# Sixteen gate projections in pairs with seven block products, in a one-core mixer block

## The chip, the cores and the metric

The kernel runs on one core of a Trainium2 chip. The metric is the device time of one execution in microseconds (us). A core has TensorE (PE in the rows; its weight loads are PEld), VectorE (DVE), ScalarE (ACT), GpSimd (POOL) and SyncE (SP), which issues most DMAs. Each engine runs its own instructions in order and waits for others by semaphores.

## The reference, cut to what matters

One transformer block on 512 tokens of width 1024, all in float32: a norm, one wide input projection, four mixers (a gated delta rule, a latent attention, a gated linear attention and an attention with forgetting), then the gates, and an MLP of width 4096. The change is in the gates:

```python
merged = 0
for i in range(4):
    gate = sigmoid(h @ w_gate[i] + b_gate[i])          # h: 512 x 1024, w_gate[i]: 1024 x 1024
    merged = merged + gate * (branches[i] @ w_branch_up[i])
x = x + rms_norm(merged @ w_out, norm_mix_post)
u = relu(rms_norm(x, norm_mlp_pre) @ w_mlp_in)         # 1024 x 4096
x = x + rms_norm((u * u) @ w_mlp_out, norm_mlp_post)
```

## The kernel before

**Numbers in two parts.** Every float32 factor of a projection is split into a high part (rounded, `fp32r`) and a low part (the rest): `split` (L157) has ScalarE cast the high part (L158) and VectorE subtract it from the source (L161). `mm3` (L257) then makes three matmuls: high by high, high by low, low by high. A projection (`proj`) of 128 output rows is 8 blocks of 128 inputs x 3 = 24 matmuls of 512 tokens.

**Tiles and buffers.** `raw_cols` loads 128 columns of a weight as 128 x 1024 (tag `raw`, four buffers); `w_split` splits them into tags `whi` and `wlo`, three buffers each. `h` is kept as `hh` and `hl`, its two parts. PSUM has two banks `acc` and six banks b0 to b5, which `ps_sm` gives out in a ring. `tmp` (L341) has four buffers of 128 x 512.

**Order.** The program is written as one sequence; a scheduler orders each engine's instructions ahead of the run, by readiness and then by place in the sequence (`tc.high_priority()` lifts a few). A tile gets a buffer of its tag when an earlier tile has let go of it.

**The gates.** `gates` (L589) makes 32 gate projections: number n is branch n % 4, rows 128 x (n // 4). The result leaves PSUM as Exp (L595), then Ln and Exp in place (L596, L597): a sigmoid. There are 11 gate buffers, so gates run up to 11 ahead of their use; two are made early, others fill TensorE's gaps in the attention parts. The loop over m = 0 to 7 (L1031) calls `gates(4 * m + 11)`, makes the branch projection of rows m (a `w_split` of `w_branch_up` and 24 matmuls, six for each branch, into four banks), multiplies each by its gate (VectorE, L1042), adds the four products on POOL (L1044, L1046) and splits the sum into `mh` and `ml`. A round from m = 2 to m = 5 is thus four gate projections and one branch projection.

**The MLP's first projection.** From its seventh block on it goes in pairs of 128-row blocks. A pair is a product of a 2 x 2 block matrix of weights (A11, A12, A21, A22, each 128 rows by 512 inputs) with a 2 x 2 block matrix of inputs (B, each 512 inputs by 256 tokens). Instead of eight block products it makes seven, of sums of blocks (Strassen's scheme in Winograd's form). `w_sums` (L1176) splits A11 and A12, then A22 into a tile `yw` of tag `y` (two buffers), then makes the four sums S1 to S4 in place in the raw weights (L1148), and splits these. `part` (L1172) makes one block product of 4 x 3 = 12 matmuls of 256 tokens. The sums T1 to T4 of the input blocks are made once, in place in `h2f`, a float32 copy of the input.

Of the kernel before, what the change touches and what calls it, by code (L numbers as in the profile page):

```python
# [121 lines left out]
def hybrid_mixer_kernel(ctx, tc, I, out):  # L122
# [891 lines left out]

    mpool = ctx.enter_context(tc.tile_pool(name="mpool", bufs=1, side="right"))

    def m_tile(name, dt):
        return mpool.tile([P, KD, S], dt, name=name, tag="mbig", bufs=2)

    mh = m_tile("mh", F32R)  # L1020
    ml = m_tile("ml", F32R)

    br_hl = {}
    for n, (i, p) in enumerate((i, p) for i in (0, 3, 2, 1) for p in range(2)):
# [2 lines left out]
        split(hi, lo, brT[i][p])  # L1027
        br_hl[i, p] = hi, lo

    banks["ring"] = ("b0", "b1", "b2", "b3", "b4", "b5")  # L1030
    for m in range(KD):  # L1031
        gates(4 * m + sum(NGATE))
        rv = raw_tile().rearrange("p (k c) -> p k c", k=KD)
        sp.dma_start(out=rv, in_=I["w_branch_up"][0].rearrange("i (k p) c -> p (i k) c", p=P)[:, :, P * m:P * m + P])
        hi, lo = w_split(rv)
        for i in range(4):
            ps = ps_sm()
            for k in range(2):
# [14 lines left out]
    def big2(name, dt):  # L1053
        return ph2.tile([P, KD, S], dt, name=name, tag="big2", bufs=2)
# [77 lines left out]
        act_sq(first[a][0], a)  # L1132

    KH = KD // 2
    B = [[h2f[:, KH * i:KH * i + KH, 256 * j:256 * j + 256] for j in range(2)] for i in range(2)]

    def rows_split(src, where):  # L1140
        wp, wb, tag = where
        hi = wp.tile([P, 1024], F32R, name="thi", tag=tag + "hi", bufs=wb).rearrange("p (k c) -> p k c", k=KH)
        lo = wp.tile([P, 1024], F32R, name="tlo", tag=tag + "lo", bufs=wb).rearrange("p (k c) -> p k c", k=KH)
        split(hi, lo, src)
        return hi, lo

    def diff(out, a, b, op=ALU.subtract):
        dve.tensor_tensor(out=out, in0=a, in1=b, op=op)  # L1148
# [12 lines left out]
    u2 += [big2("u2", F32)] + [m_tile("u2b", F32) for _ in range(2)]
    block = lambda i, j: tuple(z[:, KH * i:KH * i + KH, 256 * j:256 * j + 256] for z in (h2h, h2l))

    ring8 = [lambda: ps_sm("b0"), lambda: ps_sm("b1"), lambda: ps_sm("b2"), lambda: ps_sm("b3"), lambda: ps_sm("b4"),
             lambda: ps_sm("b5"), ps_acc, ps_acc]
    turn = [0]

    def bank():
        turn[0] += 1
        return ring8[(turn[0] - 1) % 8]()[:, 0:256]  # L1170

    def part(ps, w, t, start=True):  # L1172
        for k in range(KH):
            mm3(ps, w[0][:, k], w[1][:, k], t[0][:, k], t[1][:, k], start and k == 0, k == KH - 1)

    def w_sums(m):  # L1176

        r = [raw_cols(w1, (m + i) * P) for i in range(2)]
        A = [[v[:, KH * i:KH * i + KH] for i in range(2)] for v in r]

        def wt(name):
            return [wpool.tile([P, 1024], F32R, name="w" + z, tag="w" + z, bufs=3).rearrange("p (k c) -> p k c", k=KD)
                    for z in ("hi", "lo")]

        x = wt("x")
        split(x[0], x[1], r[0])
        z_ = ph2.tile([P, D], F32R, name="yw", tag="y", bufs=2).rearrange("p (z k c) -> p z k c", z=2, k=KH)
        z = (z_[:, 0], z_[:, 1])
        split(z[0], z[1], A[1][1])
        diff(A[1][1], A[1][0], A[1][1], ALU.add)  # L1190
        diff(A[1][0], A[0][0], A[1][0])
        diff(A[0][0], A[1][1], A[0][0])
        diff(A[0][1], A[0][1], A[0][0])
        got = []
        for pair in ((A[0][0], A[1][1]), (A[1][0], A[0][1])):
            e = wt("e")
            for i, src in enumerate(pair):
                ks = slice(KH * i, KH * i + KH)
                split(e[0][:, ks], e[1][:, ks], src)
                got.append((e[0][:, ks], e[1][:, ks]))  # L1200
        A11, A12 = [(x[0][:, KH * i:KH * i + KH], x[1][:, KH * i:KH * i + KH]) for i in range(2)]
        S2, S1, S3, S4 = got
        return A11, A12, z, S1, S2, S3, S4

    sz = lambda name: ph2.tile([P, 256], F32, name=name, tag="sz", bufs=4)
    for m in range(NPLAIN, DFF // P, 2):
        A11, A12, A22, S1, S2, S3, S4 = w_sums(m)
        o = [[u2[(m + i) // 8][:, (m + i) % 8, 256 * j:256 * j + 256] for j in range(2)] for i in range(2)]
        p1, p6, p5, p7, p3 = [bank() for _ in range(5)]
        part(p1, A11, block(0, 0))  # L1210
        s1 = sz("s1")
        with tc.high_priority():
            act.copy(out=s1, in_=p1)
        part(p6, S2, T2)
        sa = sz("sa")
        with tc.high_priority():
            diff(sa, p6, s1, ALU.add)
        part(p5, S1, T1)
        sb = sz("sb")
        with tc.high_priority():  # L1220
            diff(sb, p5, sa, ALU.add)
        part(p1, A12, block(1, 0), False)
        act.activation(out=o[0][0], in_=p1, func=AF.Relu)
        part(p7, S3, T3)
        with tc.high_priority():
            diff(o[1][1], p7, sb, ALU.add)
        part(p3, S4, block(1, 1))
        diff(o[0][1], p3, sb, ALU.add)
        part(p7, A22, T4, False)
        diff(o[1][0], p7, sa, ALU.add)  # L1230
        for i, j in ((0, 1), (1, 1), (1, 0)):
            act.activation(out=o[i][j], in_=o[i][j], func=AF.Relu)
# [81 lines left out]
```

## Time and profile before

| | us |
|---|---|
| median of 3 runs | 876.04 (874.59 to 876.36) |
| profiled execution | 875.75 |
| its span | 874.0 |
| TensorE busy in the span | 858.1 |
| VectorE busy | 529.9 |
| ScalarE busy | 441.4 |
| POOL busy | 75.6 |

The span runs from the first instruction to the last; the rest of the profiled execution's time lies around it. A busy share is an average over stages with different limits. A matmul's duration in the trace overlaps that of the next one, so the rate is read from the distance of two starts. In a row, `[x <-Y]` is idle time of that engine before the instruction, and what ended it.

### The profile page before, as it was taken

To read this page: it belongs to the slowest core of one execution; us is meant where nothing else is said; L and a number is where in the kernel's file an instruction comes from. 1 tells how busy PE (TensorE), PEld (TensorE's weight loads), DVE (VectorE), ACT (ScalarE), POOL (GpSimd) and SP (SyncE) were. 2 spreads that over 40 slices of the span, in tenths; PEclk is the share of its full clock that TensorE was granted. 3 is DMA by queue.
4 is the path that set the end of the run, shared out by engine and by line. 5 is a ranking of instruction groups with operands and counts; after the bars stand their busy time and mean duration, and the time that the engine had idled before them with its cause. 6 is when DMAs were issued, how large, how long until landed. Compare 5 with 4: busy or idle time off the path is not lost.

```text
span 874.0 us, 12382 instructions
## 1 busy us (share of the span) xinstructions
PE 858.1 (98%) x4875; PEld 728.8 (83%) x4875; DVE 529.9 (61%) x882; ACT 441.4 (50%) x788; POOL 75.6 (9%) x87
## 2 busy tenths in 40 slices
PE   7999999999999999999999999999999999999996
PEld 6988778897777777888888779999999988888885
DVE  5479698445886684444336469888888633333334
ACT  5444762433995866444453356466666632222222
POOL 3200020110000002222105100300000000000000
PEclk9999999999999999999999999999999999999999
DMA  8334153601212103333333822333344433333202
GB/s 267 86 97 118 51 95 106 145 25 49 61 49 74 48 25 97 96 97 97 97 96 97 258 56 73 87 108 97 97 109 129 148 122 97 96 97 97 73 1 96
DMA packets 123674, 83.33 MB, mean 95 GB/s; under 512 B 19472, under 2 KB 115744, under 8 KB 123616
## 3 DMA queue, kind: packets, MB, share of 16 engines
q1 hardware_dynamic: 117696, 77.03, 30.7%
q10 hardware_dynamic: 5696, 4.73, 1.8%
q8 instruction: 38, 0.62, 0.3%
q0 software_dynamic: 224, 0.79, 0.3%
q14 instruction: 20, 0.16, 0.1%
HBM read 79.63 MB, written 2.88 MB: 94 GB/s over the span
## 4 chain that ended last, share of the span: by engine, by line
PE 86%; DVE 6%; DMA 2%; ACT 2%; POOL 2%; issue 1%; ACTq 0%; SPq 0%; DVEq 0%; POOLq 0%
PE acc L259 41%; PE b L259 34%; PE b L819 2%; DMA raw<-in_w_mlp_in_dram 2%; DVE wlo L161 2%; DVE qkvT L442 1%; PE b L849 1%; PE b L840 1%; PE b L648 1%; ACT whi L158 1%; DMA raw<-in_w_in_dram 1%; POOL gate L1044 1%; POOL wlo L161 1%; PE b L495 1%; PE b L294 1%
## 5 line engine op out<-in xcount | busy, mean ns | idle before, releaser
L161 DVE TENSOR_TENSOR wlo<-raw,whi 128x1024 fp32r<-128x1024 f32 (+1 forms) x173 | 190.2, 1109 | 146.6 <-ACT whi L158 146.3
L158 ACT CAST whi<-raw 128x1024 fp32r<-128x1024 f32 (+1 forms) x175 | 159.7, 921 | 211.7 <-PE acc L259 143.6
L259 PE MATMUL acc<-hh,wlo 128*128 128x512 f32 x368 | 145.9, 396 | 0.8 <-DVE wlo L161 0.8
L259 PE MATMUL acc<-hh,whi 128*128 128x512 f32 x368 | 146.1, 397 | 0.0
L259 PE MATMUL acc<-hl,whi 128*128 128x512 f32 x368 | 145.1, 394 | 0.0
L259 PEld LDWEIGHTS acc<-hh,wlo 128*128 128x128 f32 x368 | 69.2, 188 | 16.6 <-issue 1.6
L259 PEld LDWEIGHTS acc<-hh,whi 128*128 128x128 f32 x368 | 69.2, 188 | 14.9 <-issue 1.6
L259 PEld LDWEIGHTS acc<-hl,whi 128*128 128x128 f32 x368 | 69.2, 188 | 13.7 <-issue 0.4
L259 PE MATMUL b<-whi 128*128 128x512 f32 x192 | 74.7, 389 | 0.0
L259 PE MATMUL b<-wlo,whi 128*128 128x512 f32 x192 | 74.7, 389 | 0.0
L259 PE MATMUL b<-whi,wlo 128*128 128x512 f32 x192 | 74.6, 390 | 0.0
L259 PE MATMUL b<-h2l,whi 128*128 128x256 f32 x168 | 47.7, 284 | 0.0
L259 PE MATMUL b<-h2h,wlo 128*128 128x256 f32 x168 | 47.6, 283 | 0.0
L259 PE MATMUL b<-h2h,whi 128*128 128x256 f32 x168 | 47.5, 283 | 0.0
L259 PEld LDWEIGHTS b<-whi,wlo 128*128 128x128 f32 x192 | 36.0, 188 | 7.8 <-DVE wlo L161 0.3
L259 PEld LDWEIGHTS b<-wlo,whi 128*128 128x128 f32 x192 | 36.1, 188 | 7.5
L259 PEld LDWEIGHTS b<-whi 128*128 128x128 f32 x192 | 36.0, 188 | 7.3
L1044 POOL TENSOR_TENSOR gate<-gate 128x512 f32<-128x512 f32 x16 | 22.6, 1416 | 198.3 <-DVE gate L1042 198.3
L1148 DVE TENSOR_TENSOR raw<-raw 128x512 f32<-128x512 f32 x52 | 37.3, 717 | 0.9
L259 PE MATMUL b<-thi,whi 128*128 128x256 f32 x116 | 32.8, 283 | 0.0
L259 PE MATMUL b<-tlo,whi 128*128 128x256 f32 x116 | 32.8, 283 | 0.0
L259 PE MATMUL b<-thi,wlo 128*128 128x256 f32 x116 | 32.8, 283 | 0.0
(366 smaller groups left out, 1853.0 us busy)
## 6 DMA issues: line engine op xcount, KB each, us to landing
raw<-in_w_gate_dram SPq DMA_DIRECT2D x32, 512.0 KB, 4.1
raw<-in_w_mlp_in_dram SPq DMA_DIRECT2D x32, 512.0 KB, 4.9
raw<-in_w_mlp_out_dram SPq DMA_DIRECT2D x32, 512.0 KB, 3.5
raw<-in_w_in_dram SPq DMA_DIRECT2D x23, 512.0 KB, 3.8
raw<-in_w_branch_up_dram SPq DMA_DIRECT2D x8, 512.0 KB, 4.1
raw<-in_w_out_dram SPq DMA_DIRECT2D x8, 512.0 KB, 3.6
x_t<-in_x_dram SPq DMA_DIRECT2D x4, 512.0 KB, 7.9
x<-in_x_dram ACTq DMA_DIRECT2D x1, 2048.0 KB, 12.0
```

The source lines that it names most:

```text
L158: c = act.copy(out=hi, in_=src)
L161: eng.tensor_tensor(out=lo, in0=src, in1=hi.bitcast(F32), op=ALU.subtract)
L259: pe.matmul(out=ps, lhsT=a, rhs=b, start=first and i == 0, stop=last and i == 2, skip_group_check=True)
L294: pe.transpose(out=ps[:, k * P:(k + 1) * P], in_=(src if late else sq)[:, ks], identity=ident)
L442: dve.scalar_tensor_tensor(out=y[:, sh:], in0=ps[:, 0:S - sh], scalar=vec(V_CONV + 6 * j + m), in1=y[:, sh:], op0=ALU.mult, op1=ALU.add)
L495: made.append(pe.matmul(out=ps2[e][:, js], lhsT=qkvT[2 + p][r, js], rhs=qkvT[rhs_i + p][r, js], start=j == 0, stop=j == NT - 1, skip_group ...
L648: pe.matmul(out=pv[:, j], lhsT=av[h][:, j], rhs=src[:, j], start=j == 0, stop=j == NT - 1, skip_group_check=True)
L819: pe.matmul(out=ps[:, at_[j]:at_[j] + n], lhsT=qT[e][0:rows, j * P:n], rhs=kT[e][0:rows, 0:n], start=j == js[0], stop=j == js[-1], skip_gr ...
L840: pe.transpose(out=pst[:, k * P:(k + 1) * P], in_=pr[:, k * P:(k + 1) * P], identity=ident)
L849: made.append(pe.matmul(out=psb[C * e:C * e + C, i * P:(i + 1) * P], lhsT=vt(k, 2 * p + e), rhs=pts[e][:, at_[j] + k * P:at_[j] + (k + 1) ...
L1044: pool.tensor_tensor(out=g, in0=g, in1=gts[4 * m + i - 1], op=ALU.add)
L1148: dve.tensor_tensor(out=out, in0=a, in1=b, op=op)
```

## The change

Gates 15 to 30 are made in eight pairs, (15, 16), (17, 18) and so on, with the same scheme as the MLP: the two gates' weights are the two rows of blocks, `hh` and `hl` the inputs. Gates 0 to 14 and gate 31 stay as they were. The functions of the scheme are moved ahead of both uses and shared.

- Once, before the loop over m: `hf` = `hh` + `hl` (four additions of 128 x 1024), four sums of its blocks, four splits into eight tiles `gt`. `hf` and, after it, `ml` share the one buffer of tag `mbig1`; `mh` has `mbig0`.
- For a pair: two raw weights; A11 and A12 split together, A22 split into `zg`, four sums in place, S1 to S4 split; seven products. `zg` is one pair of `tmp` tiles for all pairs, as are the intermediate results `s1`, `sa` and `sb`.
- A pair's gates leave as Exp in three pieces, then Ln and Exp as before.
- Branch projections take banks b3 to b5 in a ring; pairs take b0, b1, b2 and the two `acc`. In the MLP the pairs take the same fixed banks, where they went round all eight.
- In the MLP the four sums of input blocks are made before their splits, where they alternated; the last two relus of a pair's second half-result are one.

```diff
+GPLAIN = 15
+    def strassen_sums(f):
+        B = [[f[:, KH * i:KH * i + KH, 256 * j:256 * j + 256] for j in range(2)] for i in range(2)]
+        diff(B[0][0], B[0][1], B[0][0])
+        diff(B[0][1], B[1][1], B[0][1])
+        diff(B[1][1], B[1][1], B[0][0])
+        diff(B[1][0], B[1][0], B[1][1])
+        return B[0][0], B[0][1], B[1][1], B[1][0]
+    def strassen_weights(r, z_tile):
+        A = [[v[:, KH * i:KH * i + KH] for i in range(2)] for v in r]
...
+        x = wt()
+        split(x[0], x[1], r[0])
+        z = z_tile()
+        split(z[0], z[1], A[1][1])
+        diff(A[1][1], A[1][0], A[1][1], ALU.add)
+        diff(A[1][0], A[0][0], A[1][0])
+        diff(A[0][0], A[1][1], A[0][0])
+        diff(A[0][1], A[0][1], A[0][0])
+        for pair in ((A[0][0], A[1][1]), (A[1][0], A[0][1])):
+            e = wt()
+            for i, src in enumerate(pair):
+                ks = slice(KH * i, KH * i + KH)
+                split(e[0][:, ks], e[1][:, ks], src)
...
+    def strassen(r, bh, bl, T, dst, z_tile, sz, evict):
...
+        p1, p6, p5 = ps_acc()[:, h0], ps_sm("b0")[:, h0], ps_sm("b1")[:, h0]
+        p7, p3 = ps_acc()[:, h0], ps_sm("b2")[:, h0]
+        part(p1, A11, block(0, 0))
+        s1, sa, sb = sz("s1"), sz("sa"), sz("sb")
+        with tc.high_priority():
+            act.copy(out=s1, in_=p1)
+        part(p6, S2, T2)
+        with tc.high_priority():
+            diff(sa, p6, s1, ALU.add)
+        part(p5, S1, T1)
+        with tc.high_priority():
+            diff(sb, p5, sa, ALU.add)
+        part(p1, A12, block(1, 0), False)
+        evict(dst[0], h0, p1)
+        part(p7, S3, T3)
+        with tc.high_priority():
+            diff(dst[1][:, h1], p7, sb, ALU.add)
+        part(p3, S4, block(1, 1))
+        diff(dst[0][:, h1], p3, sb, ALU.add)
+        part(p7, A22, T4, False)
+        diff(dst[1][:, h0], p7, sa, ALU.add)
+        evict(dst[0], h1, dst[0][:, h1])
+        evict(dst[1], slice(0, 512), dst[1])
...
-        return mpool.tile([P, KD, S], dt, name=name, tag="mbig", bufs=2)
+        return mpool.tile([P, KD, S], dt, name=name, tag=f"mbig{i}", bufs=1)
+    hf = m_tile("hf", F32, 1)
+    for k in range(0, KD, 2):
+        dve.tensor_tensor(out=hf[:, k:k + 2], in0=hh[:, k:k + 2].bitcast(F32), in1=hl[:, k:k + 2].bitcast(F32), op=ALU.add)
+    gblocks = strassen_sums(hf)
+    gT = [strassen_split(b, (gstp, 1, f"gt{i}")) for i, b in enumerate(gblocks)]
...
-    banks["ring"] = ("b0", "b1", "b2", "b3", "b4", "b5")
+    banks["ring"] = ("b3", "b4", "b5")
+    zg = tmp("zg", F32R), tmp("zg", F32R)
+    def gate_pair():
+        ns = len(gts), len(gts) + 1
+        dst = [gslot(n) for n in ns]
...
+        strassen([raw_cols(I["w_gate"][0, n % 4], P * (n // 4)) for n in ns], hh, hl, (T1, T2, T3, T4), dst, z_gate,
+                 lambda name: parts_of[name], evict)
+        for g in dst:
+            act.activation(out=g, in_=g, func=AF.Ln, bias=1.0)
+            act.activation(out=g, in_=g, func=AF.Exp, scale=-1.0)
+            gts.append(g)
     for m in range(KD):
-        gates(4 * m + sum(NGATE))
+        upto = min(4 * m + sum(NGATE), 4 * KD)
+        while len(gts) < upto:
+            if len(gts) < GPLAIN or upto - len(gts) < 2:
+                gates(len(gts) + 1)
+            else:
+                gate_pair()
```

## Rows read from the trace of the kernel before

**Rows 1.** The page: span, TensorE's busy time, its granted clock by slice.

```profile
span 874.0 us, 12382 instructions
...
PE 858.1 (98%) x4875; PEld 728.8 (83%) x4875; DVE 529.9 (61%) x882; ACT 441.4 (50%) x788; POOL 75.6 (9%) x87
...
PEclk9999999999999999999999999999999999999999
```

**Rows 2.** The chain of waits: start us, us, engine, tile, line, instructions.

```profile
347.74 5.44 PE b L259 x24
353.18 21.76 PE acc L259 x96
374.94 5.44 PE b L259 x24
...
461.98 5.44 PE acc L259 x24
...
612.51 10.08 PE b L259 x84
```

**Rows 3.** Busy time by stretch: us, then each engine, clock, DMA share.

```profile
316.00:353.20 37.20, 37.20 (x197) 29.57 (x196) 20.89 (x45) 21.05 (x45) 6.11 (x4) 1.00 0.31 86
...
380.40:407.60 27.20, 27.20 (x121) 22.53 (x121) 10.56 (x10) 13.28 (x19) 4.74 (x3) 1.00 0.34 97
571.00:691.00 120.00, 120.00 (x1002) 120.00 (x1002) 100.91 (x176) 80.22 (x156) 0.00 (x0) 1.00 0.38 107
```

**Rows 4.** Timeline of TensorE where one MLP pair ends and the next starts.

```profile
571.91 0.28 PE L259 MATMUL b<-thi,yw 128*128 128x256 f32 x1
572.03 0.28 PE L259 MATMUL b<-h2h,whi 128*128 128x256 f32 x1
```

**Rows 5.** Timeline of ScalarE in the same MLP pair: A22's cast, s1, S2's cast.

```profile
572.23 0.62 ACT L158 CAST yw<-raw 128x512 fp32r<-128x512 f32 x1
572.75 0.63 ACT L1235 ACTIVATE u<-u 128x512 f32<-128x512 f32 x1
...
573.67 0.37 ACT L1213 COPY s<-b 128x256 f32<-128x256 f32 x1
...
579.97 0.62 ACT L158 CAST whi<-raw 128x512 fp32r<-128x512 f32 x1 [1.20 <-DVE raw L1148]
```

**Rows 6.** Timeline of VectorE in the same MLP pair.

```profile
573.18 0.68 DVE L161 TENSOR_TENSOR yw<-raw,yw 128x512 fp32r<-128x512 f32 x1
573.90 1.42 DVE L1148 TENSOR_TENSOR raw<-raw 128x512 f32<-128x512 f32 x2
...
579.25 0.69 DVE L1148 TENSOR_TENSOR raw<-raw 128x512 f32<-128x512 f32 x1
...
580.79 0.69 DVE L161 TENSOR_TENSOR wlo<-raw,whi 128x512 fp32r<-128x512 f32 x1
```

**Rows 7.** Timeline of VectorE and POOL in one round of the gates.

```profile
403.04 1.23 DVE L161 TENSOR_TENSOR wlo<-raw,whi 128x1024 fp32r<-128x1024 f32 x1 [4.22 <-ACT whi L158]
...
407.62 0.69 DVE L1042 TENSOR_TENSOR gate<-b,gate 128x512 f32<-128x512 f32 x1 [0.67 <-PE b L259]
408.48 2.29 DVE L161 TENSOR_TENSOR wlo<-raw,whi 128x1024 fp32r<-128x1024 f32 x1 [0.17 <-ACT whi L158]
...
409.76 2.15 POOL L1046 TENSOR_TENSOR gate<-gate 128x512 f32<-128x512 f32 x1
```

**Rows 8.** Timeline of ScalarE and VectorE around the head norm of branch 2.

```profile
279.98 1.14 ACT L158 CAST brh<-brT 128x512 fp32r<-128x512 f32 x2 [3.94 <-PE b L913]
...
285.83 0.69 DVE L161 TENSOR_TENSOR sql<-sq,sqh 128x512 fp32r<-128x512 f32 x1 [3.46 <-ACT sqh L158]
...
291.12 0.68 DVE L161 TENSOR_TENSOR brl<-brT,brh 128x512 fp32r<-128x512 f32 x1
```

**Rows 9.** The MLP's input sums (ns: least, median, most), and attention's last copy.

```profile
L1148 DVE TENSOR_TENSOR h2f<-h2f x4: 1218/1218/2064, 537.6 to 545.1; 128x1024 f32<-128x1024 f32 x4
...
330.42 0.37 ACT L853 COPY brT<-b 128x256 f32<-128x256 f32 x1 [1.04 <-PE b L849]
```

More of the change, by code (lines that the diff above doesn't have):

```diff
@@ L266, in proj, with diff, strassen_split @@
         return ps
+    KH = KD // 2
+    def diff(out, a, b, op=ALU.subtract):
+        dve.tensor_tensor(out=out, in0=a, in1=b, op=op)
+    def strassen_sums(f):
[5 more added lines that the diff above has]
+        return B[0][0], B[0][1], B[1][1], B[1][0]
+    def strassen_split(src, where):
+        wp, wb, tag = where
+        hi = wp.tile([P, 1024], F32R, name="thi", tag=tag + "hi", bufs=wb).rearrange("p (k c) -> p k c", k=KH)
+        lo = wp.tile([P, 1024], F32R, name="tlo", tag=tag + "lo", bufs=wb).rearrange("p (k c) -> p k c", k=KH)
+        split(hi, lo, src)
+        return hi, lo
@@ new lines, in strassen_weights, with wt @@
+    def strassen_weights(r, z_tile):
+        A = [[v[:, KH * i:KH * i + KH] for i in range(2)] for v in r]
+        def wt():
+            return [wpool.tile([P, 1024], F32R, name="w" + z, tag="w" + z, bufs=3).rearrange("p (k c) -> p k c", k=KD)
+                    for z in ("hi", "lo")]
+        x = wt()
[6 more added lines that the diff above has]
+        diff(A[0][1], A[0][1], A[0][0])
+        got = []
+        for pair in ((A[0][0], A[1][1]), (A[1][0], A[0][1])):
[3 more added lines that the diff above has]
+                split(e[0][:, ks], e[1][:, ks], src)
+                got.append((e[0][:, ks], e[1][:, ks]))
+        A11, A12 = [(x[0][:, KH * i:KH * i + KH], x[1][:, KH * i:KH * i + KH]) for i in range(2)]
+        S2, S1, S3, S4 = got
+        return A11, A12, z, S1, S2, S3, S4
@@ new lines, in strassen, with part @@
+    def strassen(r, bh, bl, T, dst, z_tile, sz, evict):
+        A11, A12, A22, S1, S2, S3, S4 = strassen_weights(r, z_tile)
+        T1, T2, T3, T4 = T
+        block = lambda i, j: tuple(z[:, KH * i:KH * i + KH, 256 * j:256 * j + 256] for z in (bh, bl))
+        h0, h1 = slice(0, 256), slice(256, 512)
+        def part(ps, w, t, start=True):
+            for k in range(KH):
+                mm3(ps, w[0][:, k], w[1][:, k], t[0][:, k], t[1][:, k], start and k == 0, k == KH - 1)
+        p1, p6, p5 = ps_acc()[:, h0], ps_sm("b0")[:, h0], ps_sm("b1")[:, h0]
[21 more added lines that the diff above has]
+        evict(dst[1], slice(0, 512), dst[1])
@@ L1132, in hybrid_mixer_kernel @@
         act_sq(first[a][0], a)
[L1137 to L1148, printed above, removed]
@@ L1161, in hybrid_mixer_kernel @@
[L1161 to L1174, printed above, removed]
@@ L1176, in w_sums @@
[L1176 to L1186, printed above, removed]
-        z_ = ph2.tile([P, D], F32R, name="yw", tag="y", bufs=2).rearrange("p (z k c) -> p z k c", z=2, k=KH)
[L1188 to L1203, printed above, removed]
@@ L1205, in hybrid_mixer_kernel @@
-    sz = lambda name: ph2.tile([P, 256], F32, name=name, tag="sz", bufs=4)
-    for m in range(NPLAIN, DFF // P, 2):
[L1207 to L1232, printed above, removed]
+    T4 = strassen_split(T4, spare)
@@ new lines, in hybrid_mixer_kernel, with relu_sq, z_mlp @@
+    u2 += [big2("u2", F32)] + [m_tile("u2b", F32, i) for i in range(2)]
+    def relu_sq(dst, half, src):
+        act.activation(out=dst[:, half], in_=src, func=AF.Relu)
+    sz = lambda name: ph2.tile([P, 256], F32, name=name, tag="sz", bufs=4)
+    def z_mlp():
+        z_ = ph2.tile([P, D], F32R, name="yw", tag="y", bufs=2).rearrange("p (z k c) -> p z k c", z=2, k=KH)
+        return z_[:, 0], z_[:, 1]
+    for m in range(NPLAIN, DFF // P, 2):
+        dst = [u2[(m + i) // 8][:, (m + i) % 8] for i in range(2)]
+        strassen([raw_cols(w1, (m + i) * P) for i in range(2)], h2h, h2l, (T1, T2, T3, T4), dst, z_mlp, sz,
+                 relu_sq)
```

30 lines of the change are left out of this document (17 added, 13 removed).

## The prediction

> **What bounds the kernel now.** I read the page first. The reader is to see there that TensorE is busy for 98% of an 874.0 us span, with the granted clock at its upper level (2.4 GHz) in every slice [rows 1]. So time can be won only by giving TensorE less to do, and whatever makes it wait is lost in full.
>
> Then the chain of waits, in order of time. From 347.7 us on it is TensorE alone in a regular beat: one branch projection of 24 matmuls (5.44 us), four gate projections of 96 (21.76 us), and so on; the last single gate starts at 461.98 [rows 2]. The interval between 512-column matmuls is thus 21.76/96 = 0.2267 us. Later, in the MLP, the chain shows pairs in the new form: 84 matmuls of 256 columns in 10.08 us [rows 2], 0.120 us each, as two neighbouring starts of one pair show [rows 4].
>
> By the code the pairs are gates 15 to 30: two pairs in each of the rounds m = 2, 3, 4, 5; gate 31 stays single. In the chain these are the four stretches of 21.76 us (353.18, 380.38, 407.58, 434.78: one shown, four in all).
>
> Then the table of stretches. In one round of 27.2 us VectorE works 10.56 us and ScalarE 13.28; in 120 us of MLP pairs, which is 11.9 pairs, 100.91 and 80.22, that is 8.48 and 6.74 a pair [rows 3].
>
> **TensorE's work.** A pair replaces 2 x 24 x 0.2267 = 10.88 us by 84 x 0.120 = 10.08. That is 0.80 less, 8 times: **-6.4 us**.
>
> A rule to set beside this: the Trainium skill, page "TensorE: Matmul & The Clock Gate", section "Back-to-back issue gap", puts the warm interval at N/2.4 ns plus about 2.5. That makes 109.2 and 215.8 ns, so an estimate of 1.2 us a pair and -9.5 us in all. The trace disagrees: 120 and 226.7 ns are 13.3 ns over N/2.4 both times, and a pair has 36 matmuls more to pay it. The measured intervals decide.
>
> **VectorE and ScalarE in the rounds.** Two pairs bring VectorE 2 x 8.48; the round's rest is 10.56 - 4 x 1.23 (a weight's low part without POOL beside it [rows 7]) = 5.64. Together 22.6 of some 27 us. ScalarE: 6.74 a pair, about two 512-column operations (0.62 each [rows 5]) more, since Ln and Exp on two tiles come in place of two squares; with the round's rest some 18 of 27. Both fit on average.
>
> **The wait that the change adds.** In the MLP the parts of A22 lie in a tag with two buffers. Here they lie in one pair of tiles (`zg`), made once. A22 is used by the last of the seven products, and its split must come before the sums that overwrite the raw weights in place. So nothing of S1 to S4 of the second pair of a round can be made until the first pair is through. Let T be the start of the second pair's first product. In the MLP, with T = 572.03 [rows 4], the steps stand in rows:
> - The cast of A22 starts at T + 0.20 (572.23), the moment its buffer is free, and takes 0.62 [rows 5]. There it serves the pair after; here it serves this one.
> - The low part follows at T + 0.86; 0.72 after its start come two sums of 1.42 together (573.18, 573.90), to T + 3.0 [rows 6].
> - The third sum starts there. 0.72 after it starts the cast of S2 (579.25, 579.97), which ends at T + 4.34; the low part starts 1.54 after the sum (580.79) and ends at T + 5.22 [rows 5, 6].
>
> TensorE in the meantime has the first product, to T + 1.44. The copy s1 of it starts at T + 1.64 and takes 0.37 [rows 5], then the product with A12 may run: T + 2.05 to 3.49. The product with S2 can start two matmuls at 4.34 and the rest at 5.22, so it ends at 6.42 instead of 3 x 1.44 = 4.32: a pause of **2.1 us**. If the product with S1 comes first as well (S1 needs only the first sum, so its cast can end near T + 2.95), it fills the second hole; what stays is 0.61 waiting for s1 plus some 0.3: **0.9 us**. If the products run in the written order, idle lies between 1.44 and 4.34 and the pause is 6.42 - 2.88 = **3.5 us**. The order is the scheduler's; it does take other work into holes in this kernel, so I take **1.5**, between the first two, nearer their middle than either end. Four rounds: **+6.0 us**.
>
> What else could fill the hole is the round's branch projection. It needs a weight buffer (three, of which a pair takes all), and comes after the second pair in program order. Whether a later tile gets a free buffer before an earlier one that isn't ready yet can be read off the `tmp` tag: the cast of `brh` was done by 281.1, VectorE then stood idle for 3.46 us, and yet `brl`, which needs only a `tmp` buffer, was written at 291.12, after the earlier head norm had taken its own [rows 8]. So I take it that buffers go in program order and the branch comes too late for the hole. It covers the other boundary: after the second pair come 5.44 us of branch, then 1.44 and 1.44, against the same chain of 5.22 with three gate products of 0.69 [rows 7] put in between: 7.3 of 8.3 us. Cost 0; if POOL's sums add a us (below), 0.7 at three boundaries.
>
> **Before the first pair.** VectorE gets four sums for `hf`, four for the blocks, four low parts, 128x1024 each: 12 x 1.22 = 14.6 us; ScalarE four casts. The nearest row is the same operation on `h2f` [rows 9]. In 316 to 353.2 us VectorE works 20.89 of 37.2 us [rows 3], so 16.3 are free; the last attention output is copied at 330.42 [rows 9] and the room of the new tiles is partly that of attention. If all 14.6 come at one stroke ahead of a gate's weights, TensorE has two projections in hand (10.9 us): a wait of 3.7. If they sit in the gaps: 0. I take **+0.7**.
>
> **Edits at nothing.** The MLP's sums go ahead of all splits: one sum of 1.22 sooner than a split that is needed, in a stretch where TensorE has six plain projections to do; 0, ends -0.5 and +1.2. Fixed PSUM banks in the MLP pairs: each bank is emptied before the next pair needs it; 0. One relu of 512 for two of 256: ScalarE has room; 0. Branch projections on three banks instead of six: 1.36 us of matmuls against 0.69 us of VectorE for each; 0. Two `mbig` tags for one: 0. DMAs: as many, of the same size.
>
> **Sum.** -6.4 + 6.0 + 0.7 = +0.3 on a span of 874.0, so 874.3. Around the span the profiled execution has 1.75 us (875.75), and it lies 0.29 under the median of the runs: 876.04 + 0.3 = **876.3 us**. With pauses of 0.9 to 2.1 and a start of 0 to 3.7, this case reaches from 873.2 to 881.5.
>
> **Rivals.**
> - *The hole is filled.* The scheduler gives the branch a buffer in time, or finds other work: at most 0.5 us a round. For it: TensorE's 98%, with gates lying in attention's gaps. Against it: rows 8. -6.4 + 2.0 + 0.7: **872.3**; with nothing lost, 869.6.
> - *The chain ends last and nothing is moved forward (slower).* Place: after the first pair of each round. Price 3.5 a round, and 0.7 at three boundaries: -6.4 + 14 + 2.1 + 0.7 = +10.4, **886.4**. It decides from 1.6 us a round on, where the pauses eat the 6.4. For it: ScalarE has the first pair's Exp and Ln to do just when the cast of A22 is due, and program order puts them first. Against it: in the MLP that cast slipped in between such operations at once [rows 5].
> - *VectorE becomes the bound beside POOL.* A low part took 1.23 us alone and 2.29 with POOL's 2.15 us sum beside it [rows 7]. POOL works 4.74 us in a round [rows 3]; if VectorE stands still for all of it, 22.6 + 4.74 = 27.3 against 27.2 before: no gain, +0.1 x 4 + 0.7, **877.1**. The Trainium skill has this as a rule (page "SBUF — State Buffer", section "Who interferes with whom": a VectorE instruction with two SBUF inputs and a GpSimd instruction that reads SBUF block each other whole); by that rule, this rival. The trace agrees in kind: 1.06 us longer.
>
> That the pairs don't do fewer columns isn't open: 84 x 256 against 48 x 512 stands in the code.
>
> **Chances.** The forecast 0.38, the hole filled 0.30, the chain 0.24, VectorE 0.08. A run of this kernel can tell 0.2% (1.75 us) from no change. Faster: nearly all of the second and a fifth of the first, 0.36. Slower: the chain, a third of the first, a little of the last, 0.39. Same: 0.25. Range 870.0 to 886.0: its ends are the filled hole and the chain at its price.
>
> **What would show it.** In the changed profile: 84 matmuls of about 0.120 us a pair; between the two pairs of a round TensorE idle, or its weight loads waiting for `wlo`, `whi` or the VectorE sums of `raw`, 0.9 to 2.1 us; the cast of `zg` some 0.2 us after the last product of the pair before; the order first product, A12, then S1 or S2; VectorE at 22 to 24 us a round. Wrong would be: rounds under 26 us (hole filled), branch matmuls between the two pairs of a round, or rounds over 28.5 us.

## The result, and the profile after

The changed kernel takes **889.27 us** (median of four runs, 887.12 to 890.93) where the kernel before took 876.15 on the same chip: 13.1 us more, a ratio of 1.015 [1.0132, 1.0168]. The forecast was 876.3, in a range of 870.0 to 886.0. The profiled execution is the fastest of the four: 887.12 us with a span of 885.4, 11.4 more than before.

The page of the changed kernel: span, busy times, granted clock by slice.

```profile
span 885.4 us, 13119 instructions
...
PE 857.9 (97%) x5163; PEld 737.8 (83%) x5163; DVE 598.4 (68%) x998; ACT 461.3 (52%) x827; POOL 82.6 (9%) x87
...
PEclk9999999999999998999999999999999999999999
```

Against [rows 1], VectorE works 68.5 us more, TensorE no less, and the clock has one slice that isn't at 9 (slice 16 of 22 us each: 332 to 354 us). The single gate 31 starts at 473.55 instead of 461.98 [rows 2], 11.57 later, and the end is 11.4 later: nothing was lost in the MLP.

The gates lost more than that in this execution, since it came to them early. Up to 314 us both kernels have the same instructions in the same order. TensorE's first product with the branches, before and after:

```profile
310.79 0.59 PE L259 MATMUL b<-brh,whi 128*128 128x512 f32 x1
```

```profile
307.43 0.59 PE L260 MATMUL b<-brh,whi 128*128 128x512 f32 x1
```

The changed kernel is 3.36 us ahead here. It won them in the first 25 us, which the change leaves as they were: executions differ there (e1, e2 and e10, below, with the same first part, come to this product 1.33, 1.49 and 0.17 us ahead). From this product to the first one with `w_out`, behind the last gates (478.15 before, 489.83 after), TensorE takes 182.40 us instead of 167.36: **15.0 us** more. Below, "by the rows" means this stretch against its 167.36. A difference of a us or two between medians can come from the first 25 us alone.

**Before the first pair.** The chain of waits of the changed kernel, 328 to 355 us (start us, us, engine, tile, line, instructions):

```profile
328.01 0.83 PE b L935 x12
...
328.92 4.63 DVE hf L1110 x4
...
340.97 1.14 DVE tlo L162
342.11 0.61 DVE gate L1164
...
342.79 2.17 POOL gate L1166
...
345.04 2.14 POOL gate L1168
...
347.21 0.70 ACT gate L681
...
347.95 6.92 PE acc L260 x23
```

VectorE had less room there than [rows 3] suggest. The kernel before from attention's last copy [rows 9] to 353.2, in the columns us, then busy time of PE, PEld, DVE, ACT, POOL, granted clock, DMA share, GB/s:

```profile
330.40:353.20 22.80, 22.80 (x100) 18.62 (x101) 10.17 (x11) 13.22 (x20) 6.11 (x4) 1.00 0.42 116
```

Read the chain as a relay. `hf` can start only when attention's last matmuls are through, since it takes the place of attention's tiles. Then VectorE makes sums and low parts in one stroke of 13 us. The last gate product of branch rows 0 stands behind them in VectorE's queue, POOL's two sums wait for that product, a gate buffer comes free only with them, and the Exp that empties TensorE's bank `acc` needs such a buffer. In the kernel before, POOL was through with all three sums of branch rows 0 at 338.67; here it begins the second of them at 342.79.

TensorE's timeline of the same stretch shows what it costs (in brackets the idle time ahead):

```profile
339.56 0.39 PE L260 MATMUL b<-brl,whi 128*128 128x512 f32 x1
342.76 0.50 PE L260 MATMUL b<-brh,whi 128*128 128x512 f32 x1 [2.82 <-DVE gate L1164]
...
345.74 0.80 PE L260 MATMUL acc<-hh,whi 128*128 128x512 f32 x1 [2.24 <-ACT gate L681]
...
347.95 0.58 PE L260 MATMUL acc<-hh,whi 128*128 128x256 f32 x1 [0.99 <-ACT gate L681]
...
349.40 0.63 PE L260 MATMUL acc<-hl,whi 128*128 128x512 f32 x1
349.82 0.63 PE L260 MATMUL acc<-hh,wlo 128*128 128x512 f32 x1
```

Starts 3.20, 2.64 and 1.62 us apart, and after them seven matmuls 0.43 apart (349.40, 349.82), not 0.2267. The table of stretches, in the same columns, has VectorE busy without a break:

```profile
338.00:348.00 10.00, 3.95 (x14) 2.14 (x12) 10.00 (x8) 4.52 (x6) 4.31 (x2) 0.83 0.07 21
```

**Inside a round.** The first pair of a round, then the second, behind one branch projection; TensorE's waits in the round from 386.17 to 415.23:

```profile
389.85 0.38 PE L260 MATMUL b<-thi,wlo 128*128 128x256 f32 x1 [0.82 <-DVE wlo L162]
...
391.55 0.39 PE L260 MATMUL b<-thi,wlo 128*128 128x256 f32 x1 [0.25 <-DVE wlo L162]
...
400.59 0.38 PE L260 MATMUL acc<-hh,whi 128*128 128x256 f32 x1 [0.75 <-ACT s L335]
...
402.70 0.39 PE L260 MATMUL b<-thi,wlo 128*128 128x256 f32 x1 [0.18 <-DVE wlo L162]
```

The last two are the forecast pause: the second pair's first product starts at T = 398.24, then come A12, and S1 and S2 in turn, and the three products behind the first end at 405.43 where T + 5.76 = 404.00 would be without a wait: **1.43 us**, 0.91 of them for the copy s1 (a gap of 1.03 at 400.59). The first two lie at the boundary that was to cost nothing. VectorE's timeline there:

```profile
385.73 1.18 DVE L274 TENSOR_TENSOR raw<-raw 128x512 f32<-128x512 f32 x1
386.83 0.68 DVE L1164 TENSOR_TENSOR gate<-b,gate 128x512 f32<-128x512 f32 x1
387.44 0.68 DVE L274 TENSOR_TENSOR raw<-raw 128x512 f32<-128x512 f32 x1
388.03 4.06 DVE L162 TENSOR_TENSOR wlo<-raw,whi 128x512 fp32r<-128x512 f32 x3
```

Gate products and the pair's sums take turns in the queue, and three low parts take 4.06 where four took 3.15 in the same round (403.16, no POOL beside them). One round by the table of stretches:

```profile
386.17:415.23 29.06, 27.00 (x194) 24.95 (x193) 24.39 (x37) 17.38 (x30) 4.95 (x4) 1.00 0.34 91
```

29.06 us against 27.2 before and 25.6 of matmuls: 3.46 of waits, 1.43 of them between the pairs and 2.03 at the other boundary.

### The profile page after: what moved, and what is told of

The parts are those of the page before. It is cut to its first block, busy times and chain, and to the rows that moved or that the text cites. A ratio compares the mean times of both kernels' runs of the same rounds, so it can differ in the third digit from the quotient of the medians.

```text
span 885.4 us, 13119 instructions
## 1 busy us (share of the span) xinstructions
PE 857.9 (97%) x5163; PEld 737.8 (83%) x5163; DVE 598.4 (68%) x998; ACT 461.3 (52%) x827; POOL 82.6 (9%) x87
## 4 chain that ended last, share of the span: by engine, by line
PE 82%; DVE 12%; ACT 3%; POOL 2%; issue 1%; DMA 0%; DVEq 0%; POOLq 0%; ACTq 0%
PE acc L260 38%; PE b L260 33%; DVE wlo L162 3%; PE b L905 2%; DVE raw L274 2%; DVE gate L1164 1%; DVE qkvT L528 1%; PE b L935 1%; PE b L926 1%; PE b L734 1%; POOL gate L1168 1%; ACT whi L159 1%; POOL gate L1166 1%; DVE zg L162 1%; PE b L380 1%
## 5 line engine op out<-in xcount | busy, mean ns | idle before, releaser
L162 DVE TENSOR_TENSOR wlo<-raw,whi 128x1024 fp32r<-128x1024 f32 (+1 forms) x197 | 206.1, 1060 | 90.7 <-ACT whi L159 90.1
L260 PE MATMUL acc<-hh,whi 128*128 128x512 f32 (+1 forms) x304 | 116.3, 383 | 6.3 <-ACT gate L681 3.2
L260 PE MATMUL acc<-hh,wlo 128*128 128x512 f32 (+1 forms) x304 | 114.6, 377 | 0.8 <-DVE wlo L162 0.8
L260 PE MATMUL acc<-hl,whi 128*128 128x512 f32 (+1 forms) x304 | 114.0, 375 | 0.0
L274 DVE TENSOR_TENSOR raw<-raw 128x512 f32<-128x512 f32 x84 | 61.6, 733 | 1.4
L260 PE MATMUL b<-thi,wlo 128*128 128x256 f32 x168 | 48.2, 289 | 3.8 <-DVE wlo L162 3.7
L260 PE MATMUL b<-thi,whi 128*128 128x256 f32 x168 | 47.4, 284 | 0.0
L260 PE MATMUL acc<-h2h,whi 128*128 128x256 f32 (+1 forms) x136 | 40.4, 297 | 0.0
L260 PE MATMUL acc<-h2l,whi 128*128 128x256 f32 (+1 forms) x136 | 40.2, 295 | 0.0
L260 PE MATMUL acc<-h2h,wlo 128*128 128x256 f32 (+1 forms) x136 | 40.2, 295 | 0.0
## 6 DMA issues: line engine op xcount, KB each, us to landing
x<-in_x_dram ACTq DMA_DIRECT2D x1, 2048.0 KB, 10.9
```

The costliest lines, as they stand in the source:

```text
L162: eng.tensor_tensor(out=lo, in0=src, in1=hi.bitcast(F32), op=ALU.subtract)
L260: pe.matmul(out=ps, lhsT=a, rhs=b, start=first and i == 0, stop=last and i == 2, skip_group_check=True)
```

## The experiments

Times are medians; the kernel before, run beside each, lay at 875.4 to 876.2. "Gap" is the distance of two neighbouring starts on TensorE.

### Start or rounds: one half alone

**e1_prep_only**: all gates single; `hf`, sums and splits are made for nothing.

```diff
-GPLAIN = 15
+GPLAIN = 32
```

> All 32 gates single, as before the change; the sums of the input's blocks are still made (and used by nothing), and branch projections keep their three banks. Theory: half of the loss comes ahead of the first pair, where VectorE makes 14.6 us of sums and low parts at one stroke while TensorE waits for gate products and gate buffers behind them. Then this costs 5.8 us over the kernel before (876.2): 881 to 883, and the rounds keep 27.2 us. Rival: what delays the start is the first pair's own weight sums; then this costs under 2 us, up to 878.

**e2_no_prep**: the pairs without the preparation (blocks of `hh` and `hl` stand in for T1 to T4, so the pairs' gates aren't the reference's).

```diff
-    hf = m_tile("hf", F32, 1)
...
-    gT = [strassen_split(b, (gstp, 1, f"gt{i}")) for i, b in enumerate(gblocks)]
+    gT = [tuple(z[:, KH * i:KH * i + KH, 256 * j:256 * j + 256] for z in (hh, hl)) for i in range(2) for j in range(2)]
```

> The changed kernel without hf, its four sums and their splits: the pairs multiply by blocks of hh and hl in their place, so the gates 15 to 30 are left wrong. Theory: 5.8 us less than the changed kernel (889.3), 882.5 to 884.5, and the rounds stay at 29.06 us. Rival (the three banks or the first pair's weights delay the start): 887 or more.

e1: 884.57, +8.7 (ratio 1.0098 [1.0083, 1.0114]). e2: 880.30, +4.45 (1.0055 [1.0038, 1.0072]). Together 13.15, the whole loss. Both miss what was expected: the start costs more than the 5.8 put down to it, the rounds less. By the rows e1 loses 10.5 and e2 5.7, 1.2 more than the changed kernel's 15.0. TensorE in e1 has the gaps of the changed kernel, and then thirteen matmuls, not seven, 0.42 to 0.43 apart, which is that 1.2 (granted clock 0.67 in 348 to 360 us, so in part at the lower level, 1.2 GHz):

```profile
344.81 0.50 PE L260 MATMUL b<-brh,whi 128*128 128x512 f32 x1 [2.82 <-DVE gate L1164]
...
347.78 0.80 PE L260 MATMUL acc<-hh,whi 128*128 128x512 f32 x1 [2.24 <-ACT gate L681]
...
350.00 0.79 PE L260 MATMUL acc<-hh,whi 128*128 128x512 f32 x1 [0.99 <-ACT gate L681]
350.59 0.63 PE L260 MATMUL acc<-hl,whi 128*128 128x512 f32 x1
351.01 0.63 PE L260 MATMUL acc<-hh,wlo 128*128 128x512 f32 x1
```

And e2's round, 29.07 us, has the same four waits:

```profile
382.35 0.38 PE L260 MATMUL b<-hh,wlo 128*128 128x256 f32 x1 [0.82 <-DVE wlo L162]
384.04 0.39 PE L260 MATMUL b<-hh,wlo 128*128 128x256 f32 x1 [0.25 <-DVE wlo L162]
393.10 0.39 PE L260 MATMUL acc<-hh,whi 128*128 128x256 f32 x1 [0.76 <-ACT s L335]
395.20 0.39 PE L260 MATMUL b<-hh,wlo 128*128 128x256 f32 x1 [0.17 <-DVE wlo L162]
```

### The rounds

**e3_two_zg**: two pairs of `zg` tiles in turn; for the room, `s1` and `sa` share one.

```diff
-    zg = tmp("zg", F32R), tmp("zg", F32R)
+    zgs = [(tmp("zg", F32R), tmp("zg", F32R)), (tmp("zg", F32R), bslot("zg", F32R))]
```

> A22's parts get two buffers in turn (s1 and sa share one tile to make the room). Theory: both waits of a round come from the single zg, since S1 to S4 can't be made before the pair ahead is through; with two, a round comes down from 29.06 to 25.8 to 26.6 us, some 3 us each in three rounds and 1.4 in the other: 878 to 880.5. Rival (VectorE's amount of work, 22.6 us and POOL's 4.7 beside it, sets the round): a round stays at 28 or more, 886 or more.

890.50 (1.016 [1.0126, 1.0193]): nothing won, a miss. The waits for S1 and S2 are gone, rounds are 27.6 and 28.9, and what waits now is the product with A22. TensorE, and VectorE's queue ahead of it:

```profile
398.27 0.39 PE L260 MATMUL acc<-thi,zg 128*128 128x256 f32 x1 [0.70 <-DVE gate L274]
```

```profile
395.46 1.82 DVE L162 TENSOR_TENSOR wlo<-raw,whi 128x1024 fp32r<-128x1024 f32 x2
397.20 0.68 DVE L274 TENSOR_TENSOR raw<-raw 128x512 f32<-128x512 f32 x1
397.80 0.42 DVE L274 TENSOR_TENSOR gate<-acc,sb 128x256 f32<-128x256 f32 x1
```

The bank p7 holds S3's product, must be read (`gate<-acc,sb`), and takes A22's on top; the read stands behind low parts and sums that the second `zg` allowed to come forward. A buffer gave the next pair's work room to get in the way of this one's. (That `s1` and `sa` now share a tile wasn't tested by itself; no wait in these rounds is put down to it.)

**e4_no_pool**: POOL's three sums left out in rounds 2 to 5 (their merged sums lack three branches).

```diff
-            if i % 2:
+            if i % 2 and not 2 <= m <= 5:
```

> The changed kernel without POOL's three sums in the rounds m = 2 to 5, so the branches aren't added up there. Theory: of the wait after the branch projection (2.0 us) most is VectorE slowed beside POOL (a sum 1.18 instead of 0.68, three low parts 4.06 instead of 1.9): it falls to 0.3 at three boundaries, a round to some 27.4 us, 884 to 885. Rival (the four gate products put in between are what delays it): at most 0.5 a round less, 887.5 or more.

884.59 (1.0094 [1.0072, 1.0115]), 4.7 less than the changed kernel, as expected, in rounds of 27.17 with 2.5 us less of VectorE:

```profile
389.43:416.60 27.17, 26.25 (x193) 24.83 (x192) 21.85 (x37) 17.27 (x30) 0.00 (x0) 1.00 0.36 98
```

The waits at the branch's boundary are all but gone, those between the pairs stand (gaps of 1.03 and 0.45). So 1.89 of the 2.03 are POOL's.

**e12_no_pool_two_zg**: both edits at once.

> The changed kernel with two pairs of zg in turn (as in e3) and without POOL's sums in rounds m = 2 to 5 (as in e4; the merged sum of those rounds lacks three of its branches). Theory (what the rounds lose is VectorE's queue: POOL stretches it, so that the early read of p7 comes late, and the single zg adds its pause): with both gone rounds come to 25.6 + 0.4 to 0.8, about 26.2, some 1 us under e4's 27.17 each; 884.59 - 4 = 880.6. Rival (the read of p7 stands behind the next pair's sums with or without POOL): rounds stay at 27 and more, 884 or more.

884.30 (1.0097 [1.0072, 1.0122]): the rival. Rounds of 26.4 and 27.6; waits of 0.82 and 1.97 at the A22 product, the second behind a `zg` cast that had waited 2.06 us for the raw weight's DMA. With both known causes away the next two limits come up, the read of p7 and the four raw buffers.

**e5_alternate**: one pair, then two single gates a round.

```diff
-            if len(gts) < GPLAIN or upto - len(gts) < 2:
+            if len(gts) < GPLAIN or upto - len(gts) != 4:
```

> In the rounds m = 2 to 5 only the first two gates go as a pair, the other two single; the start is as in the changed kernel. TensorE's work in a round is 10.08 + 10.88 + 5.44 = 26.4 us. Theory: the waits come from sums that can be made only once the pair ahead is through, and that stand on VectorE between gate products and beside POOL; 10.9 us of single gates after each pair cover that chain of 5 to 8 us. Then a round is 26.4 to 26.9 us instead of 29.06, and what stays is the start's 8.7: 882 to 883.5. Rival (each pair brings its own wait, whatever comes after it): a round of 28 us or more, 886.5 or more.

884.93 (1.0114 [1.0097, 1.0131]), more than expected, in rounds of 27.12: 10.88 + 10.08 + 5.44 = 26.40 of matmuls and one wait of 0.72, for the read of p7:

```profile
427.09 0.39 PE L260 MATMUL acc<-thi,zg 128*128 128x256 f32 x1 [0.45 <-DVE gate L274]
```

### The start: order, banks, amount, stroke

**e6_prep_later** puts `hf`, sums and splits behind round 0's products and POOL sums; **e7_later_alternate** has the edit of e5 as well; **e8_prep_six_banks** is e1 with the branch's six banks given back.

```diff
+        if m == 0:
+            hf = m_tile("hf", F32, 1)
...
+            gT[:] = [strassen_split(b, (gstp, 1, f"gt{i}")) for i, b in enumerate(strassen_sums(hf))]
+            ml = m_tile("ml", F32R, 1)
```

```diff
-    banks["ring"] = ("b3", "b4", "b5")
+    banks["ring"] = ("b0", "b1", "b2", "b3", "b4", "b5")
```

> The changed kernel with hf, its sums and splits placed after the gate products and POOL sums of the round m = 0, so that VectorE takes those first. Theory: the start loses 8.7 us since branch 0's gate products stand behind 14.6 us of sums on VectorE, and with them PSUM banks and gate buffers; behind the products, the start loses 2 to 4 us: 883 to 885. Rival: the amount of VectorE work decides, whatever its order; 888 or more.

> Both of these edits: four pairs, and the sums behind round m = 0's products. Theory: the gains add up, the start loses 2 to 4 us and four rounds gain 0.3 to 0.8 each against 27.2: 875.5 to 879, no more than 3 over the kernel before. Rival: 882 or more.

> As e1 (all gates single, the sums made for nothing), but branch projections go round six banks as before the change. If the first wait of the start (3.2 us at a branch projection) is for one of three banks, it is gone: 880 to 882. If it is for VectorE's products as such, gates then wait for their buffers just as long: 884 to 885, as e1 (884.6).

e6: 887.30 (1.014 [1.0125, 1.0155]), e7: 881.41 (1.0072 [1.0057, 1.0087]), e8: 886.61 (1.0132 [1.0113, 1.0151]). With 4.45 for the rounds taken off e6's 11.8, the start still loses 7.3: round 0's products are now in time, but the stroke holds up the next things in the queue, a weight's low part (a gap of 2.14 at 350.43) and the first pair's (2.03 at 361.05). The three banks aren't it: with six the loss is 11.1 (by the rows 10.9, e1 10.5). All three lie outside what was expected, e6 and e7 between theory and rival, e8 above both.

**e9_sums_only** (no splits) and **e10_hf_only** (no block sums either) cut e1's stroke down; the edit of e9 beside GPLAIN = 32:

```diff
-    gT = [strassen_split(b, (gstp, 1, f"gt{i}")) for i, b in enumerate(gblocks)]
+    gT = [tuple(z[:, KH * i:KH * i + KH, 256 * j:256 * j + 256] for z in (hh, hl)) for i in range(2) for j in range(2)]
```

> GPLAIN = 32 (all gates single) with hf and the four block sums, but without the eight splits: 8 x 1.22 = 9.8 us of VectorE ahead of the loop instead of 14.6, and no casts. Nothing of it is used. Theory (amount: TensorE loses what VectorE's stroke exceeds its lead by; the full 14.6 us lost 8.7, so the lead is 5.9): 9.8 - 5.9 = 3.9, about 879.7, and less if the fall of the granted clock (some 14 matmuls at 0.43 us, 2.9 us of e1's loss) goes away with the long pause: 877 to 880. Rival (the room, the three banks or the order of buffers): as long as e1, 883 to 885.

> GPLAIN = 32 with only the four additions of hf: 4.9 us of VectorE, nothing of it used. Theory (amount): under the lead of 5.9, so no loss: 875.5 to 876.5. Rival (room, banks, order of buffers, since hf still stands ahead of ml and the three banks stay): 880 or more.

e9: 881.33 (1.0073 [1.0048, 1.0097]), e10: 875.31 (0.9992 [0.998, 1.0005]). Losses of 5.2 and none. e9 lies between theory and rival. Losses that grow with the stroke sound like amount, but e9's rows show another path. TensorE's one long gap (4.78) ends at 345.63, VectorE's stroke at 343.74 already, and then VectorE stands idle for 3.15 us, up to 346.88; what the gap waits for is POOL, on a single sum of 5.58 us. POOL's, then ScalarE's timeline:

```profile
339.27 5.58 POOL L1166 TENSOR_TENSOR gate<-gate 128x512 f32<-128x512 f32 x1 [17.32 <-DVE gate L1164]
344.93 1.27 POOL L1168 TENSOR_TENSOR gate<-gate 128x512 f32<-128x512 f32 x1
```

```profile
344.89 0.69 ACT L681 ACTIVATE gate<-acc,vneg 128x512 f32<-128x512 f32 x1 [5.73 <-POOL gate L1166]
```

**e16_prep_no_pool**: e1 without POOL's sums in round 0.

```diff
-            if i % 2:
+            if i % 2 and m:
```

> e1 (all gates single, hf, sums and splits made for nothing) without POOL's three sums in round m = 0 (that round's merged sum lacks three branches). Theory (the stroke holds up the gate products of branch 0, POOL's sums come after them at 2.15 instead of 1.29 us, a gate buffer comes free only behind these, and TensorE's bank acc waits for it): the gaps of 2.63 and 1.63 us go, and with them most of the half-speed matmuls; of 8.7 lost 3 to 4.5 stay: 879 to 880.5. Rival (VectorE's amount of work alone): 883 or more, as e1.

881.34 (1.0065 [1.0049, 1.0081]): 3.2 us less than e1 (3.5 by the rows), a little less than forecast. TensorE's waits for the Exp of `gate` are gone; the wait for the gate product itself stays, one for a low part is new, and the slow matmuls stay too:

```profile
345.81 0.50 PE L260 MATMUL b<-brh,whi 128*128 128x512 f32 x1 [2.36 <-DVE gate L1164]
...
348.07 0.79 PE L260 MATMUL acc<-hh,wlo 128*128 128x512 f32 x1 [0.65 <-DVE wlo L162]
348.67 0.63 PE L260 MATMUL acc<-hh,whi 128*128 128x512 f32 x1
349.09 0.63 PE L260 MATMUL acc<-hl,whi 128*128 128x512 f32 x1
```

**e11_spread**: more VectorE work (19.3 us by rows, not 14.6), in four pieces; each block sum is made from the parts in two `tmp` halves.

```diff
+    pieces = [lambda: piece(1, ((hh, 1, 1), (hh, 0, 1), (hl, 1, 1), (hl, 0, 1))),
+              lambda: piece(0, ((hh, 0, 1), (hh, 0, 0), (hl, 0, 1), (hl, 0, 0))),
+              lambda: piece(2, ((hh, 1, 1), ta, (hl, 1, 1))),
+              lambda: piece(3, ((hh, 1, 0), ta, (hl, 1, 0)))]
...
                 gates(len(gts) + 1)
+                if m == 1:
+                    pieces.pop(0)()
```

> GPLAIN = 32; hf is left out, each block sum is made from the parts of hh and hl in two tmp halves, 20 sums of 128x512 (0.69 us) and 8 low parts of 0.69, together 19.3 us of VectorE, in four pieces of 4.1 to 5.5 us, one behind each of the gates 11 to 14. Nothing of it is used. Theory (the amount counts, not the place): 19.3 us against 16.3 of free VectorE and the lead of 5.9: a loss of 9 or more, 885 or more. Rival (the single stroke is what hurts; pieces lie in VectorE's gaps): a loss under 3, 876 to 879.

876.56 (1.0016 [1.0004, 1.0028]): 0.4 lost by the medians, 0.4 to 2.5 by the interval (two gaps on TensorE, 0.78 and 1.25, are left). The theory of the amount has fallen. One thing beside the cutting differs from e1: `hf` is gone, so the first six of the 28 operations need no room of attention's and run at 291 to 301 us already. The other 22, 17 us by their rows and still more than e1's 14.6, lie in 337 to 357. VectorE works 10.00 of 10.00 us in 338 to 348, as in the changed kernel, and TensorE 9.60, not 3.95. The gate product has got its place between two pieces' sums:

```profile
338.93 0.68 DVE L274 TENSOR_TENSOR ta<-hh 128x512 f32<-128x512 f32 x1
339.53 0.68 DVE L1183 TENSOR_TENSOR gate<-b,gate 128x512 f32<-128x512 f32 x1
340.13 0.68 DVE L274 TENSOR_TENSOR ta<-ta,hl 128x512 f32<-128x512 f32 x1
```

### Both put together

**e13_spread_pairs** is e11's start with the pairs; **e14_spread_alt_late** adds e5's order and puts A12's product behind S4's, to give the read of p7 another 1.44 us; **e15_spread_two_zg_late** does so with e3's two `zg`.

```diff
+        if late:
+            part(p1, A12, block(1, 0), False)
+            evict(dst[0], h0, p1)
         part(p7, A22, T4, False)
```

> The changed kernel with the block sums made in four pieces as in e11 (first pair and rounds as in the changed kernel). Theory (start and rounds add up: the start now costs 0.4, the rounds 4.45 as in e2): 876.1 + 0.4 + 4.5 = 881.0. Rival (without the pause in front, the first pair comes while VectorE still makes the last piece, and the loss moves there): 884 and more.

> Pieces as in e13, one pair and then two single gates a round as in e5, and the product with A12 moved behind the product with S4, so that two products (2.88 us) instead of one lie between the end of S3's product and the A22 product, which waits for VectorE's read of p7 (0.72 us in e5). Theory: rounds of 26.4 instead of 27.12, four of them 0.8 us under the 27.2 of before: 876.1 + 0.4 - 3.2 = 873.3. Rival (the read of p7 comes as much later, since VectorE's queue and not the order of products sets it, or s1 and its bank p1 are now held longer): rounds of 27.1, 876.2.

> Pieces as in e13, two pairs a round, two zg in turn as in e3, and A12's product behind S4's. Theory (what e3's rounds lost stood at the A22 product, for the read of p7): rounds of 26.0 to 26.6 for 29.06 of the changed kernel: 876.1 + 0.4 - 4 x 0.9 = 872.9, and up to 875. Rival (VectorE's 24 to 25 us a round beside POOL, or the raw weights' DMAs, are the bound): rounds of 27.5 or more, 878 and more.

893.03 (1.0196 [1.0179, 1.0213]), 886.25 (1.0117 [1.0101, 1.0134]) and 888.91 (1.0157 [1.0137, 1.0177]): all three forecasts missed, the rivals of e13 and e15, and e14 slower than its rival too. With a pair right behind the pieces, its four sums and six low parts join the same queue. TensorE in e13:

```profile
357.44 0.39 PE L260 MATMUL acc<-hh,whi 128*128 128x256 f32 x1 [1.44 <-ACT s L335]
364.60 0.58 PE L260 MATMUL b<-thi,whi 128*128 128x256 f32 x1 [5.46 <-ACT whi L159]
```

Behind the second pause 23 matmuls of 256 columns stand 0.21 apart instead of 0.12 (granted clock 0.54 in 364.6 to 372 us), 2.1 us more.

But e14's rounds are 26.74 without a wait of over 0.33: moving A12 did cure p7. e15's two pairs a round still wait (1.75 at 400.94, 1.87 at 441.28, both at A22), and the move has a price there: three times a gap of 1.12 ahead of the second pair, for ScalarE's Exp, which empties the bank of the A12 product that now comes later.

**e17_three_pairs_wide**: as e14, the pieces one in two gates and pairs from round 3 on (three pairs). **e18_pair_last**: four pairs, each the last of its round.

```diff
-GPLAIN = 15
+GPLAIN = 19
...
-                if m == 1:
+                if len(gts) in (12, 14, 16, 18):
```

> As e14, but the four pieces stand behind gates 11, 13, 15 and 17, one in two gates, and pairs begin in round m = 3: three pairs (19 and 20, 23 and 24, 27 and 28). Theory (e13 and e14 lost their 12 us where the first pair's four sums and six low parts queued behind the pieces; with 10.9 us of TensorE work for each 5.5 us piece VectorE is through in time): no pause of more than 1 us before or in the first pair, three rounds of 26.74 as in e14 instead of 27.2: 876.2 + 0.4 - 1.4 = 875.2. Rival (the first pair's chain is late by itself, whatever stands ahead of it): a gap of 3 us or more at the first product with a block sum, 878 to 882.

> As e17, with pieces behind gates 11, 13, 15 and 16 and the pair as the last of each round, four pairs from gates 17 and 18 on. Theory: the first pair begins two gates (10.9 us) after that of e14, one piece stands close ahead of it; two full gates lie ahead of each pair and a branch behind it, so its sums have time: rounds of 26.4 to 26.8, 876.2 + 0.4 - 4 x 0.46 = 874.8, and up to 877 if the last piece stands in the first pair's way. Rival (as in e17): 879 or more.

e17: **875.61** (1.0004 [0.9992, 1.0016]), no change, as expected; no gap above 0.8 us from 336 to 475. e18: 878.40 (1.0034 [1.0022, 1.0046]), between theory and rival: one pause of 3.11 at the first pair, behind the last piece. The rounds of e17, then e18:

```profile
402.54:429.32 26.78, 26.73 (x157) 23.65 (x156) 17.05 (x23) 15.41 (x25) 4.58 (x3) 1.00 0.35 99
```

```profile
406.01:432.43 26.42, 26.42 (x158) 23.60 (x157) 17.95 (x24) 15.06 (x25) 5.11 (x3) 1.00 0.35 99
```

e18's round is the 26.40 of matmuls to 0.02. So a pair's 0.80 us can be had, once a round; three times 0.42 to 0.8 is what such a version saves, and the start, 0.4 to 2.5 in e11, can cost it again. None of the versions beats the kernel before.

## Why the prediction was wrong

- *TensorE's -6.4*: right. 84 matmuls at 0.120 us, and e18's rounds show the saving whole.
- *The pause between the pairs, 1.5 a round*: right, 1.43, with the order that was named. That it came so near is partly luck: 1.5 was picked between 0.9 and 2.1, and 0.91 of the 1.43 stands at the copy s1, where the working had 0.61. Its reading as the price of the single `zg` held only in part: e3 took that away and the next wait, for p7, cost as much.
- *The second boundary, 0 (0.7 with POOL)*: wrong, 2.03. The step counted 7.3 us of VectorE against 8.3 of TensorE and took POOL for one us, which by this count fills the 8.3 and costs nothing; the 0.7 has no working. e4 shows that POOL beside it is the difference (1.89). The third rival had the mechanism and priced it by the round (27.3 of 27.2); it acts at the boundary, on the sums that TensorE waits for, while VectorE is idle elsewhere in the round. By steps the rounds come to -6.4 + 4 x 1.43 + 3 x 2.03 = +5.4; e2 has +4.45 by the medians and +5.7 by the rows, so nothing large is left out.
- *The start, +0.7 (0 to 3.7)*: the step that failed most; e1 has +8.7. The upper end asked how long TensorE's weights would last. The stroke hit another queue mate: a gate product, behind which hang POOL's sums, the gate buffers and the bank `acc`. e16 puts 3.2 us on POOL's part, e11 shows that such work in pieces costs 0.4 to 2.5, e1's rows show thirteen matmuls at 0.43 instead of 0.23 after the pauses, 13 x 0.20 = 2.6. The free 16.3 us [rows 3] were also misread: they count from 316 us on, and `hf` has to wait for attention, whose last copy is at 330.42 [rows 9]. From there VectorE has 22.80 - 10.17 = 12.6 us free (the stretch shown above), less than 14.6. That is the smaller part: e11 gets 17 us into about the same stretch. Free time in a sum says nothing of whose turn it is.
- *Edits at nothing*: held for the MLP; taking the three banks back won nothing at the start either (e8), and in the rounds it wasn't tested.
- *The case's own range*, 873.2 to 881.5: its upper end adds up to 881.7 (-6.4 + 8.4 + 3.7), still far under 889.27.
- *The slower rival*, 886.4, came near the time and not the place: its price of 3.5 between the pairs was 1.43. The order "nothing moved forward" was not seen.

What stays open: why e8 loses 2.4 more than e1 (by the rows only 0.5 of it stands at the gates), how much of e11's gain comes from the cutting and how much from the six early sums, and what e17's start costs by itself: its three savings of 0.42 are no more than e11's interval allows for the pieces.

## What to carry to other kernels

A block of work for an engine with free time is priced by what stands behind it in that engine's queue, and by what each of these holds (a bank, a buffer, another engine's sum), not by its share of the stretch; and free time counts only from when the block can start. Cut it into pieces between the items that others wait for, and keep its first user a few us away: 19.3 us in pieces cost 0.4 to 2.5, 14.6 in one stroke 8.7, and the pieces with a pair close behind 12. Where a saving is 0.8 us at a time, look first for the wait that will come next when the present one is gone.

## What the runs showed of the hardware

- Which of POOL and VectorE waits for the other is not fixed. POOL's 128x512 sum took 1.29 us by itself and 2.17 in the changed kernel (342.79), where two low parts of VectorE took 4.50 instead of 2.4 at the same time: both were late. In e9 VectorE's two sums and two low parts ran back to back at their usual 1.22 each to 343.7, and POOL's sum, begun at 339.27, ended at 344.85, 1.1 us after them: POOL alone was late, by 4.3. The Trainium skill, page "SBUF — State Buffer", section "Who interferes with whom", has the two block each other whole when the VectorE instruction has two SBUF inputs, as here; the rows agree, what one is late being the time that the other takes. They show besides, in e9, that POOL's turn came only when VectorE's queue paused.
- After e9's single pause of 4.78 us the next seven matmuls of 512 columns stood 0.42 to 0.43 us apart; after e13's of 5.74, 23 of 256 columns stood 0.21 apart; after e18's of 3.11 the clock stayed at 1.00 and 256 columns took 0.12, the full rate. In e1 the pauses that ended in half rate were 3.20, 2.63 and 1.63 in a row. TensorE's idle time thus cost more than itself: 2.6 us on top of e1's pauses, 2.1 on top of e13's.
- The first 25 us differ between executions that have the same instructions there: in the profiles of the changed kernel, e1, e2 and e10 TensorE came out of them 3.36, 1.33, 1.49 and 0.17 us ahead of the kernel before.
